# Row-wise infinity norm: another plan of tail loads, and the first load from two queues

## The chip, the cores and the metric

The kernel runs on one core of a Trainium2 chip. The metric is the device time of one execution in microseconds, lower being better. Three executions of the kernel before gave 629.21, 629.24 and 629.35 us; their median is 629.24 us.

## The reference

The input is a float32 matrix of 8192 rows and 8192 columns. The output has one float32 for each row: the largest absolute value in it.

```python
def setup_inputs():
    return {"x": np.random.randn(8192, 8192).astype(np.float32)}

def reference(x: np.ndarray) -> np.ndarray:
    return np.linalg.norm(x, ord=np.inf, axis=1)
```

The kernel reads 268.44 MB from HBM once and writes 32 KB.

## The kernel before

Loads are issued by SyncE's DMA queue, the reductions run on VectorE, a few combinations of partial results on GpSimd. ScalarE and TensorE do nothing.

**Two parts of the matrix.** The last 18 x 128 rows are the tail (`ROWS = 18`): each of the 128 partitions holds 18 consecutive rows, one after another, so that a partition's part is a line of 147456 elements. All rows before are the big part, in 23 steps: in each step a partition gets two whole rows, so a load has 128 partitions x 16384 elements (8 MB). `x_big` and `x_tail` are these views.

**The ring.** The loads go into one SBUF buffer, `ring`, of 3 x 16384 elements per partition, with 2048 elements apart from it (`APART`) for the pieces of the last row. `Pieces.room` hands out places in the ring one after another and begins again at the start when the rest is too short. A load may only start when the reductions that read its place are done, and when the reduction eight loads before is done, since the eight semaphores (`SEMS`) each count one load at a time. So up to three big loads are in SBUF: one being reduced and two landing or waiting on the queue.

**Loads and reductions.** `Pieces.load` (the DMA is line 90 of the profile) issues a load and adds 16 to its semaphore when it has landed. `Pieces.reduce` (line 108) issues the `tensor_reduce` with the absolute maximum over each row, or piece of a row, of the load. Its first instruction waits for the load's semaphore; VectorE takes the loads in their order. In the big part one instruction reduces two rows into `res_big`.

**The plan of the tail.** `tail_loads` cuts the line of 18 rows into loads that become smaller toward the end. It works backward from the last load, whose width is `FIRST` columns, with a linear cost for a load (`LOAD`, us per column and us per load) and for a reduction (`REDUCE`); each earlier load is made about as wide as lets its reduction be done when the next load has landed. Widths are multiples of `GRAIN` = 64; `SNAP` moves a cut to the end of a row where that is near. The last piece of row 16 is loaded late, just before the last piece of row 17. In the kernel before the tail has 25 loads, the first of 16384 columns, the last ones of 1984, 1920, 1664, 1472, 1280 and 1152 columns.

**Partial results.** A row in several pieces gets a partial maximum for each. For rows 0 to 16 GpSimd combines them (line 205) into `res_tail`. For row 17 the partial results are written behind the last piece in the ring, so that the last reduction reads 1152 + 4 elements and needs no combination.

**The end.** Three stores go out on SyncE's queue. `early` (line 218, `res_big`) and `middle` (line 222, the first 16 tail rows) wait for the reduction before last. The final store (line 235, rows 16 and 17 of the tail) waits for GpSimd's last combination and for the last of six one-element memsets (`IDLE`, line 216), which stand behind the last reduction on VectorE.

Of the kernel before, what the change touches and what calls it, by code (L numbers as in the profile page):

```python
# [7 lines left out]
P = 128  # L8
# [3 lines left out]
SEMS = 8  # L12


LOAD = (1.1775e-3, 0.075)
REDUCE = (1.0417e-3, 0.060)
ROWS = 18
FIRST = 1152
SNAP = 0.7
GRAIN = 64  # L20

IDLE = 6


def tail_loads(n_cols, big):

    slack = 0.0
    lag = REDUCE[0] * FIRST + REDUCE[1]
    loads = []
    end = ROWS * n_cols

    def take(top, bottom, most):
        nonlocal slack
        w = 0  # L40
        n = 0
        while True:

            n += 1
            start = max(bottom, (top - 1) // n_cols * n_cols - (n - 1) * n_cols)
            fit = int((lag + slack - REDUCE[1] * n) / REDUCE[0])
            w = max(w, min(fit, top - start) // GRAIN * GRAIN)
            if fit <= top - start or start <= bottom:
                break
        w = max(GRAIN, min(w, most, top - bottom))  # L50
        row = (top - w + n_cols - 1) // n_cols * n_cols
        if top - row >= SNAP * w or (w == most and top > row):
            w = top - row
        n = (top - 1) // n_cols - (top - w) // n_cols + 1
        slack += (LOAD[0] - REDUCE[0]) * w + LOAD[1] - REDUCE[1] * n
        loads.append((top - w, w))
        return top - w

    ends = [take(end, end - n_cols, FIRST), take(end - n_cols, end - 2 * n_cols, n_cols)]
    for top, bottom in zip(ends, (end - n_cols, 0)):  # L60
        while top > bottom:
            top = take(top, bottom, big)
    return loads[::-1]


class Pieces:
# [7 lines left out]
    def __init__(self, tc, ring):  # L74
        self.tc, self.nc, self.ring, self.head = tc, tc.nc, ring, 0
        self.sems = [tc.alloc_semaphore(f"loaded{i}") for i in range(SEMS)]
        self.started = self.reduced = 0
        self.last = []

    def room(self, w):  # L80
        if self.head + w > RING:
            self.head = 0
        at = self.head
        self.head += w
        return at

    def load(self, at, w, src):
        i = self.started
        self.started += 1
        ins = self.nc.sync.dma_start(out=self.ring[:, at : at + w], in_=src)  # L90
        ins.then_inc(self.sems[i % SEMS], 16)
        self.tc.no_tile_sem_insts.add(ins.ins.name)
        self.tc.declare_no_dep(ins.ins, group="loads", reason="a reduction stands in between")
        self.tc.add_to_no_dep_group("loads", ins.ins)
        if i >= SEMS:
            self.tc.add_manual_dep(
                ins.ins,
                self.last[i - SEMS].name,
                mybir.DependencyInfo(mybir.DependencyClass.Sync, mybir.DependencyReason.DATA),
                reason="the semaphore counts one load at a time",  # L100
            )

    def reduce(self, pairs):

        i = self.reduced
        self.reduced += 1
        for k, (dst, src) in enumerate(pairs):
            ins = self.nc.vector.tensor_reduce(  # L108
                out=dst,
                in_=src,  # L110
                axis=mybir.AxisListType.X,
                op=mybir.AluOpType.max,
                apply_absolute_value=True,
            )
            if k:
                self.tc.keep_in_program_order(ins)
            else:
                ins.wait_op(self.sems[i % SEMS], 16 * (i // SEMS + 1), "sem-ge")
            self.tc.declare_no_dep(ins.ins, group="loads", reason="waits on the load's semaphore")
        self.last.append(ins.ins)  # L120
        return ins
# [3 lines left out]
def kernel(  # L125
# [5 lines left out]
    nc = tc.nc  # L131
# [3 lines left out]
    tail = tail_loads(n_cols, R * n_cols)  # L135
    split = n_rows - ROWS * P
    n_big = split // (R * P)
# [8 lines left out]
    res_big = single.tile([P, n_big, R], f32)  # L146
    res_tail = single.tile([P, ROWS], f32)
    idle = single.tile([1, IDLE], f32)
    pieces = Pieces(tc, ring)

    for t in range(n_big):
        at = pieces.room(R * n_cols)
# [6 lines left out]
    for i, (start, w) in enumerate(tail):  # L159
        c = 0  # L160
        while c < w:
            row = (start + c) // n_cols
            n = min(w - c, (row + 1) * n_cols - start - c)
            parts.append((row, i, c, n))
            c += n
    of_row = [[q for q in parts if q[0] == row] for row in range(ROWS)]

    spots, behind, dst = {}, {}, {}  # L170
    at = RING
    for row, own in enumerate(of_row):
        if row == ROWS - 1:
            spots[own[-1][1]] = at
# [13 lines left out]
    for i, (start, w) in enumerate(tail):  # L188
        at = spots[i] if i in spots else pieces.room(w)
# [7 lines left out]
        )  # L197
        for row in range(ROWS - 1):
            if len(of_row[row]) > 1 and of_row[row][-1][1] == i:
                best = dst[of_row[row][0]]  # L200
                more = [dst[q] for q in of_row[row][1:]]
                while more:
# [3 lines left out]
                        out=to,  # L206
# [7 lines left out]
    tc.declare_fence(done.ins, group="loads")  # L214
    for i in range(IDLE):
        tc.keep_in_program_order(nc.vector.memset(idle[:, i : i + 1], 0.0))  # L216

    early = nc.sync.dma_start(
        out=out[:split].rearrange("(p q) -> p q", p=P), in_=res_big.rearrange("p t r -> p (t r)")
    )  # L220
    out_tail = out[split:].rearrange("(p r) -> p r", p=P)
    middle = nc.sync.dma_start(out=out_tail[:, : ROWS - 2], in_=res_tail[:, : ROWS - 2])
    for store in (early, middle):
        tc.add_manual_dep(
            store.ins,
# [2 lines left out]
            reason="not beside the last load",  # L228
# [37 lines left out]
```

## Time and profile before

| what | value |
|---|---|
| median of three runs | 629.24 us |
| time of the profiled execution | 629.17 us |
| its span in the profile | 627.4 us |
| VectorE busy | 551.9 us, 88% of the span, 62 instructions |
| reduction of 128x16384 (23 of them) | 17220 ns each |
| reduction of 128x8192 (9 in the tail) | 8677 ns each |
| last reduction, 128x1156 | 1347 ns |
| first load issued, first reduction starts | 0.72 us, 22.58 us |
| last load issued, final store issued | 609.34 us, 625.09 us |

The span is the time between the first and the last instruction that the profile records; the execution's own time is 1.77 us longer. Each DMA load is one instruction on SyncE's queue; its data moves on the core's 16 DMA engines, and the profile also records their packets. A reduction's busy time contains a part that overlaps with the next reduction: consecutive reductions start about 0.08 us before the one ahead has ended.

### The profile page before, as it was taken

To read this page: it belongs to the slowest core of one execution; us is meant where nothing else is said; L and a number is where in the kernel's file an instruction comes from. 1 tells how busy PE (TensorE), PEld (TensorE's weight loads), DVE (VectorE), ACT (ScalarE), POOL (GpSimd) and SP (SyncE) were. 2 spreads that over 40 slices of the span, in tenths; PEclk is the share of its full clock that TensorE was granted. 3 is DMA by queue.
4 is the path that set the end of the run, shared out by engine and by line. 5 is a ranking of instruction groups with operands and counts; after the bars stand their busy time and mean duration, and the time that the engine had idled before them with its cause. 6 is when DMAs were issued, how large, how long until landed. Compare 5 with 4: busy or idle time off the path is not lost.

```text
span 627.4 us, 170 instructions
## 1 busy us (share of the span) xinstructions
DVE 551.9 (88%) x62; POOL 2.9 (0%) x13
## 2 busy tenths in 40 slices
DVE  0588988889988889888898888988889899999998
POOL 0000000000000000000000000000000000000000
DMA  9999999999999999999999999999999999999997
GB/s 401 401 468 401 468 401 468 401 468 401 468 401 468 401 468 401 468 401 468 401 468 401 468 401 464 405 455 414 443 410 440 452 401 429 432 440 429 419 423 298
DMA packets 7345, 268.48 MB, mean 428 GB/s; under 512 B 1200, under 2 KB 1200, under 8 KB 1968
## 3 DMA queue, kind: packets, MB, share of 16 engines
q1 hardware_dynamic: 7344, 268.47, 99.3%
q14 instruction: 1, 0.01, 0.0%
HBM read 268.44 MB, written 0.03 MB: 428 GB/s over the span
## 4 chain that ended last, share of the span: by engine, by line
DMA 57%; DVE 42%; issue 0%; DVEq 0%; SPq 0%
DMA ring<-in_x_dram 57%; DVE res_big L108 22%; DVE parts L108 11%; DVE res_tail L108 8%; DVE ring L108 1%; DVEq L261 0%; SPq L90 0%; DVE idle L216 0%
## 5 line engine op out<-in xcount | busy, mean ns | idle before, releaser
L108 DVE TENSOR_REDUCE res_big<-ring 128x2 f32<-128x16384 f32 x23 | 396.1, 17220 | 69.4 <-DMA ring<-in_x_dram 69.4
L108 DVE TENSOR_REDUCE res_tail<-ring 128x1 f32<-128x8192 f32 (+1 forms) x10 | 78.9, 7944 | 2.1 <-DMA ring<-in_x_dram 2.1
L108 DVE TENSOR_REDUCE parts<-ring 128x1 f32<-128x3520 f32 (+17 forms) x19 | 69.8, 3735 | 1.7 <-DMA ring<-in_x_dram 1.7
L108 DVE TENSOR_REDUCE ring<-ring 128x1 f32<-128x1984 f32 (+3 forms) x4 | 7.7, 1975 | 0.0
L205 POOL TENSOR_SCALAR res_tail<-parts 128x1 f32<-128x1 f32 x8 | 2.3, 289 | 614.1 <-DVE parts L108 614.1
L205 POOL TENSOR_SCALAR parts<-parts 128x1 f32<-128x1 f32 x1 | 0.4, 354 | 7.0 <-DVE parts L108 7.0
L250 POOL MEMSET const-bfloat16-1.0<- 128x1 bf16 x1 | 0.1, 102 | 0.0
L250 POOL MEMSET const-uint8-127<- 128x1 uint8 x1 | 0.1, 101 | 0.0
L250 POOL MEMSET const-float32-0.0<- 128x1 f32 x1 | 0.1, 98 | 0.2 <-issue 0.2
L250 POOL MEMSET const-float32-1.0<- 128x1 f32 x1 | 0.1, 98 | 0.0
L216 DVE MEMSET idle<- 1x1 f32 x6 | 0.1, 59 | 0.0
## 6 DMA issues: line engine op xcount, KB each, us to landing
ring<-in_x_dram SPq DMA_DIRECT2D x3, 4096.0 KB, 41.9
ring<-in_x_dram SPq DMA_DIRECT2D x1, 7488.0 KB, 31.1
ring<-in_x_dram SPq DMA_DIRECT2D x1, 6368.0 KB, 35.4
ring<-in_x_dram SPq DMA_DIRECT2D x1, 5920.0 KB, 40.8
ring<-in_x_dram SPq DMA_DIRECT2D x1, 4800.0 KB, 32.8
ring<-in_x_dram SPq DMA_DIRECT2D x1, 3488.0 KB, 40.4
ring<-in_x_dram SPq DMA_DIRECT2D x1, 3104.0 KB, 39.2
ring<-in_x_dram SPq DMA_DIRECT2D x1, 2944.0 KB, 40.8
```

Of the source, the lines that this page charges most:

```text
L108: ins = self.nc.vector.tensor_reduce(out=dst, in_=src, axis=mybir.AxisListType.X, op=mybir.AluOpType.max, apply_absolute_value=True,)
L205: combined = nc.gpsimd.tensor_scalar(out=to, in0=best, scalar1=two[0], scalar2=two[1] if len(two) == 2 else None, op0=mybir.AluOpType.max, ...
L216: tc.keep_in_program_order(nc.vector.memset(idle[:, i : i + 1], 0.0))
L250: nc = _bacc.Bacc("TRN2", target_bir_lowering=False, num_devices=1)
```

## The change

Five things change:

- The constants of the plan: `LOAD` 0.075 to 0.073, `FIRST` 1152 to 768, `SNAP` 0.7 to 0.6, and a new `SPARE` of 0.08 us which is taken from the time that every load but the last is allowed for its reduction. The tail then has 29 loads, the first of 16384 columns, the last ones of 1600, 1472, 1344, 1152, 1024, 896, 768 and 704 columns.
- The first load of the kernel is issued as two DMAs: partitions 0 to 63 from SyncE's queue and partitions 64 to 127 from ScalarE's. Both add 16 to the same semaphore, and the counts to wait for are kept in `due`.
- `early` and `middle` are issued by ScalarE's queue. The final store stays on SyncE's.
- `IDLE` goes from six memsets to two.
- The number of instructions follows: 60 reductions for 56, one more combination on GpSimd, four more loads on SyncE's queue. Rows 16 and 17 come in 5 and 7 pieces, where they had 4 and 5, so the last reduction reads 704 + 6 elements.

```diff
-LOAD = (1.1775e-3, 0.075)
+LOAD = (1.1775e-3, 0.073)
 REDUCE = (1.0417e-3, 0.060)
+SPARE = 0.08
 ROWS = 18
-FIRST = 1152
-SNAP = 0.7
+FIRST = 768
+SNAP = 0.6
 GRAIN = 64
 
-IDLE = 6
+IDLE = 2
...
+        spare = SPARE if loads else 0
         while True:
...
-            fit = int((lag + slack - REDUCE[1] * n) / REDUCE[0])
+            fit = int((lag + slack - spare - REDUCE[1] * n) / REDUCE[0])
...
-        ins = self.nc.sync.dma_start(out=self.ring[:, at : at + w], in_=src)
-        ins.then_inc(self.sems[i % SEMS], 16)
-        self.tc.no_tile_sem_insts.add(ins.ins.name)
...
+        dst = self.ring[:, at : at + w]
+        queues = [(self.nc.sync, slice(0, P))]
+        if i == 0:
+
+            queues = [(self.nc.sync, slice(0, P // 2)), (self.nc.scalar, slice(P // 2, P))]
+        for queue, rows in queues:
+            ins = queue.dma_start(out=dst[rows], in_=src[rows])
+            ins.then_inc(self.sems[i % SEMS], 16)
+            self.counts[i % SEMS] += 16
+            self.tc.no_tile_sem_insts.add(ins.ins.name)
...
+        self.due.append(self.counts[i % SEMS])
...
-                ins.wait_op(self.sems[i % SEMS], 16 * (i // SEMS + 1), "sem-ge")
+                ins.wait_op(self.sems[i % SEMS], self.due[i], "sem-ge")
...
-    early = nc.sync.dma_start(
+    early = nc.scalar.dma_start(
...
-    middle = nc.sync.dma_start(out=out_tail[:, : ROWS - 2], in_=res_tail[:, : ROWS - 2])
+    middle = nc.scalar.dma_start(
+        out=out_tail[:, : ROWS - 2], in_=res_tail[:, : ROWS - 2]
+    )
```

More of the change, by code (lines that the diff above doesn't have):

```diff
@@ L78, in __init__ @@
         self.last = []
+        self.counts, self.due = [0] * SEMS, []
     def room(self, w):
@@ L89, in load @@
         self.started += 1
-        ins = self.nc.sync.dma_start(out=self.ring[:, at : at + w], in_=src)
-        ins.then_inc(self.sems[i % SEMS], 16)
-        self.tc.no_tile_sem_insts.add(ins.ins.name)
-        self.tc.declare_no_dep(ins.ins, group="loads", reason="a reduction stands in between")
-        self.tc.add_to_no_dep_group("loads", ins.ins)
+        dst = self.ring[:, at : at + w]
[7 more added lines that the diff above has]
+            self.tc.no_tile_sem_insts.add(ins.ins.name)
+            self.tc.declare_no_dep(ins.ins, group="loads", reason="a reduction stands in between")
+            self.tc.add_to_no_dep_group("loads", ins.ins)
+        self.due.append(self.counts[i % SEMS])
         if i >= SEMS:
```

## The prediction, made before the changed kernel was run

> **What bounds the kernel now.** I read the busy shares, then the DMA queues, then the chain of waits, then the groups of instructions with their waits, and last the stretches at both ends. From the page (parts 1 to 3):
>
> ```profile
> DVE 551.9 (88%) x62; POOL 2.9 (0%) x13
> ...
> DMA  9999999999999999999999999999999999999997
> ...
> q1 hardware_dynamic: 7344, 268.47, 99.3%
> ...
> HBM read 268.44 MB, written 0.03 MB: 428 GB/s over the span
> ```
>
> The DMA engines are busy in every slice (99.3% of the span), VectorE in 88%: the stream of loads is the bound. In the packet records a row of 64 KB takes one DMA engine 2.418 us, which is 27.1 GB/s, and 16 engines make 433.6 GB/s. The 268.44 MB then need 619.1 us at least; the span is 627.4, so 8.3 us lie outside the steady stream. A whole load of 128x16384 has eight such rows per engine, 8 x 2.418 = 19.34 us, and successive landings are indeed 19.35 us apart.
>
> The chain of waits, in order of time, says where the bound changes hands:
>
> ```profile
> 1.15 40.73 DMA ring<-in_x_dram
> 41.88 0.02 issue
> 41.91 17.23 DVE res_big L108
> ...
> 465.53 31.14 DMA ring<-in_x_dram
> 496.67 0.02 issue
> 496.69 7.22 DVE parts L108
> 503.91 17.19 DVE res_tail L108 x2
> 521.10 8.65 DVE parts L108 x2
> 529.75 34.37 DVE res_tail L108 x4
> 564.12 50.70 DVE parts L108 x14
> 614.83 7.58 DVE ring L108 x4
> 622.40 0.06 DVE parts L108
> ```
>
> Up to 496.67 the chain alternates between a load and its reduction (VectorE waits about 2.1 us for each load); from there to the end VectorE never waits. But it is only just late: the last load is issued at 609.34, lands 14.3 us later at 623.59, and its reduction starts at 623.72. So the DMA engines and VectorE end together: the widths of the tail loads are chosen so that each reduction is done about when the next load lands.
>
> The start, in stretches (width, VectorE and GpSimd busy, clock, DMA share, GB/s; a packet counts where it starts):
>
> ```profile
> 1.00:1.50 0.50, 0.00 (x0) 0.00 (x0) 1.00 0.00 0
> 1.50:2.00 0.50, 0.00 (x0) 0.00 (x0) 1.00 4.02 1311
> 2.00:2.50 0.50, 0.00 (x0) 0.00 (x0) 1.00 1.80 655
> 2.50:3.00 0.50, 0.00 (x0) 0.00 (x0) 1.00 0.31 131
> ```
>
> 1311 x 0.5 us is ten rows of 64 KB, 655 x 0.5 five, 131 x 0.5 one: the 16 engines start their first rows from 1.74 to 2.67 us, though SyncE issued at 0.72. These first rows take 2.51 to 3.49 us, not 2.42. Load 0 lands at 22.56.
>
> [...]
>
> **The change part by part.** The sum is made on the profiled execution (629.17 us, span 627.4, 1.8 outside it); the median, 629.24, is 0.07 above it.
>
> *Tail plan.* Intervals between landings in the tail fit 1.1766 ns per column plus 0.073 us per load (most within 0.008 us). Four more loads, with the same columns: the last landing moves by 4 x 0.073 = +0.29 us, to 623.88. The last reduction goes from 1156 columns (1.347 us) to 710; rows of 8192 (8.676) and 1156 give 1.0416 ns per column and 0.143, so 0.883 us: -0.464. VectorE's lag behind the last landing goes from 0.13 to 0.09. I stepped through both plans load by load (start = later of landing + 0.024 and VectorE free; 0.061 us net per reduction): before ends at 625.07 (the profile has 625.06), after at 624.85. **-0.22 us.** All other reductions, four more of them, are in that recurrence; their cover is the same 0.1 us lag behind the loads. GpSimd has one more combination (0.29 us) earlier, hidden: the last of them still follows the reduction before last and ends some 0.4 us before the final store.
>
> *Fillers, six to two.* The final store waits for the last memset. They start 0.007 to 0.01 us apart (625.004 to 625.039); four fewer: **-0.03 us**.
>
> *Stores on ScalarE's queue.* Both wait for the reduction before last, now at about 624.05. Issues of 0.35 and 0.43 us then run to about 624.9. On SyncE they would end right where the final store is due (624.87); on ScalarE nothing is queued behind them. They land after 1.5 and 1.7 us, the second at about 626.2, under the final store (624.87 + 1.5 = 626.35). If the cover of 0.15 fails, up to +0.2. I take 0. SyncE's issues in the tail (0.33 each, four more) wait for reductions as before, with several loads queued ahead of them (landing comes 14 us after the last issue): 0.
>
> *First load in two halves.* ScalarE leaves the opening barrier at 0.66 and is free at 0.73, against SyncE's issue at 0.72, so both queues fill together, and the issue on ScalarE (some 0.38 us) delays nobody. Load 1 sits behind the first half on SyncE's queue. The first reduction waits for both halves. What this does to the stream isn't shown in the trace; I bound it.
> - Lower end: each queue has 64 rows to describe instead of 128. If that is what staggers the starts (0.93 us), half of it goes: -0.46. If the queues share the describing, 0. I take -0.3 in this case.
> - Upper end: every engine alternates rows of the two halves. When all 16 engines have a row of the lower half, [...] each row takes twice 2.418; then all turn to the upper half[...]. Load 0 takes 128 / 8 x 2.418 = 38.7 us instead of 19.35: +19.3. [...] The spread of 0.93 us in the starts is small against a row of 4.8, so I see little that pulls the engines apart. I take **+17.5**[...].
>
> A delay of load 0 isn't absorbed later: each following load comes through queues that never run empty (99.3%), so every landing, and with it the end, moves by the delay of the slowest engine. VectorE just waits longer once.
>
> Sum with contention: -0.22 - 0.03 + 17.5 = +17.2 us, 646.4 from the median. Without: -0.25 - 0.3 = -0.55, 628.7.
>
> **The rivals.**
> 1. *Contention[...]* (57%): full, about 646.4 (own range 643 to 649; 42%), or partial, where engines get into opposite phase after some rows (631 to 643; 15%). For it: the bound is the DMA engines[...]. It decides from small doses: one row in eight at half speed on the slowest engine costs 2.4 us, more than the tail gives back. Against: [...] the two queues fill within 0.02 us of each other[...].
> 2. *No contention, small gain* (37%): 628.7, between 628.0 and 629.3. The queue interleaves finely or the engines fall into opposite phase at once. For it: the tail arithmetic is exact to 0.01 us on the kernel before, and the start has only 0.93 us of stagger to win.
> 3. *A larger gain at the start* (6%): the first rows at full speed from 1.74 for all engines would let load 0 land up to 1.1 us sooner (5.29 where the last first row ends, less 1.74 + 2.42); with the tail -1.35, 627.9.
> 4. That the tail plan misses its aim, with VectorE waiting for loads again, is inside all of these: each wait would show as at most 0.1 us.
>
> **How the numbers follow.** A measurement of this kernel can tell about 0.2%, 1.26 us, from no change: 627.98 to 630.50 count as the same. Contention in any dose lies above it (57%); the small gain lies within it (37%); the larger one under it (6%). The forecast is that of the likeliest case, 646.4. The range from 628.3 to 649.0 reaches from most of the small gain to full contention plus 2.6 us, and leaves out the larger gain, the edge of the small one and a worse contention, together under 2 in 10.
>
> **What would show it.** Contention: in the stretch from 1.7 to 40 us the DMA rate is near half of 433 GB/s, rows of the first load last up to 4.8 us in the packet records, and the first reduction starts near 40 us instead of 22.58; later landings are again 19.35 us apart. No contention: first reduction at 22.1 to 22.6. In both, the last reduction (128x710) takes 0.88 us, starts about 0.1 us after its landing, and VectorE has no idle time after its wait near 496 (or that plus the shift). I am wrong on the main point if load 0 lands by 23 us; on the tail, if VectorE waits for loads in its last 100 us, or if ScalarE's second store lands after the final one.

## The result, and the profile after

The changed kernel takes 649.68 us (median of four runs, 649.05 to 649.97) against 629.30 (629.21 to 629.45) beside it: a ratio of 1.0322, 95% interval 1.0307 to 1.0338, so 20.4 us slower. The profiled execution took 649.81 us with a span of 648.0. The forecast was 646.4 with a range to 649.0: the direction was right, and so was the place of the loss (the rows of the first load at about half their rate); the size was 3.2 us too small and the range ended 0.7 us too low.

The page of the changed kernel, parts 1 to 3:

```profile
DVE 552.1 (85%) x62; POOL 3.2 (0%) x14
...
DMA  9979999999999999998999999999899999999997
GB/s 194 259 259 453 445 396 453 453 396 445 453 433 409 453 445 396 453 453 388 453 453 417 425 453 441 400 453 453 388 453 432 417 439 432 419 444 421 425 423 292
...
q1 hardware_dynamic: 7568, 264.25, 96.2%
q10 hardware_dynamic: 368, 4.23, 3.1%
...
HBM read 268.44 MB, written 0.03 MB: 414 GB/s over the span
```

VectorE has as much work as before (551.9 us there). The new queue, q10, is ScalarE's: 4.19 MB of it are its half of the first load. The row to look at is GB/s: in the first three of 40 slices (16.2 us each) it is 194 to 259, while the busy row above it still shows 9, 9 and 7. In the kernel before it was 401 or more in every slice but the last:

```profile
GB/s 401 401 468 401 468 401 468 401 468 401 468 401 468 401 468 401 468 401 468 401 468 401 468 401 464 405 455 414 443 410 440 452 401 429 432 440 429 419 423 298
```

A row that takes twice as long (about 4.9 us instead of 2.42, below) is recorded as busy for all of that time: in the stretch from 10 to 20 us a DMA share of 0.98 goes with 210 GB/s here, and one of 1.04 with 452 in the kernel before. So a full busy row doesn't say how fast bytes move.

The changed kernel in finer stretches (columns as in the prediction: width, VectorE and GpSimd busy, clock, DMA share, GB/s):

```profile
1.50:2.00 0.50, 0.00 (x0) 0.00 (x0) 1.00 0.00 0
2.00:2.50 0.50, 0.00 (x0) 0.00 (x0) 1.00 9.39 1966
2.50:3.00 0.50, 0.00 (x0) 0.00 (x0) 1.00 0.65 131
...
5.00:10.00 5.00, 0.00 (x0) 0.00 (x0) 1.00 0.98 210
10.00:20.00 10.00, 0.00 (x0) 0.00 (x0) 1.00 0.98 210
20.00:30.00 10.00, 0.00 (x0) 0.00 (x0) 1.00 0.98 210
30.00:40.00 10.00, 0.00 (x0) 0.00 (x0) 1.00 0.98 210
46.00:60.00 14.00, 14.00 (x1) 0.00 (x0) 1.00 1.04 449
```

And one stretch of the kernel before:

```profile
10.00:20.00 10.00, 0.00 (x0) 0.00 (x0) 1.00 1.04 452
```

Until 40 us the rate is 210 GB/s, half of what follows, with a DMA share of 0.98. The first rows now start at 2.05 us, where they started at 1.74. In the packet records 16 rows of SyncE's half come first, as many as there are engines, then 16 of ScalarE's, and so on, eight turns, each row about 4.9 us long (means of 4.89 to 4.92, 5.02 in the first turn). The engines begin a turn within 1.1 us of one another, and this spread doesn't grow: both halves are being loaded at the same time for only a fifth of the time. From 44 us on, rows take 2.42 us again.

The chain of waits, in order of time:

```profile
0.72 42.44 DMA ring<-in_x_dram
43.16 0.03 issue
43.19 17.22 DVE res_big L119
60.41 1.71 another core or an unknown queue
62.12 0.02 issue
62.14 17.23 DVE res_big L119
79.37 0.02 issue
79.39 40.78 DMA ring<-in_x_dram
...
485.76 31.15 DMA ring<-in_x_dram
516.91 0.02 issue
516.93 6.75 DVE parts L119
...
643.46 0.06 DVE parts L119
643.52 0.70 issue
644.22 0.91 DVEq L274
645.12 0.01 DVE idle L227 x2
```

The end of the same chain before:

```profile
625.06 0.04 DVE idle L216 x6
```

(What ends at 62.12 is the wait for the second load, though the chain can't name its queue.) The first reduction starts at 43.19 instead of 22.58, the second at 62.14 instead of 41.91: 20.2 us late. After that the rhythm is the old one (40.78 for two loads in the chain, as before), and the last reduction ends at 645.12 instead of 625.06, 20.06 us late. So the loss stands complete at 62 us, and the tail gives back 0.2 us.

### The profile page after: what moved, and what is told of

It reads as the page before. It is cut to its first block, busy times and chain, and to the rows that moved or that the text cites. A ratio compares the mean times of both kernels' runs of the same rounds, so it can differ in the third digit from the quotient of the medians.

```text
span 648.0 us, 176 instructions
## 1 busy us (share of the span) xinstructions
DVE 552.1 (85%) x62; POOL 3.2 (0%) x14
## 4 chain that ended last, share of the span: by engine, by line
DMA 55%; DVE 43%; another core or an unknown queue 0%; issue 0%; DVEq 0%
DMA ring<-in_x_dram 55%; DVE res_big L119 24%; DVE parts L119 12%; DVE res_tail L119 7%; DVE ring L119 1%; DVEq L274 0%; DVE idle L227 0%
## 5 line engine op out<-in xcount | busy, mean ns | idle before, releaser
L119 DVE TENSOR_REDUCE parts<-ring 128x1 f32<-128x3136 f32 (+18 forms) x22 | 78.5, 3639 | 1.2 <-DMA ring<-in_x_dram 1.2
L119 DVE TENSOR_REDUCE res_tail<-ring 128x1 f32<-128x8192 f32 (+1 forms) x9 | 69.8, 7812 | 2.1 <-DMA ring<-in_x_dram 2.1
L119 DVE TENSOR_REDUCE ring<-ring 128x1 f32<-128x1600 f32 (+5 forms) x6 | 8.3, 1444 | 0.0
```

What stands on the lines that cost most here:

```text
L119: ins = self.nc.vector.tensor_reduce(out=dst, in_=src, axis=mybir.AxisListType.X, op=mybir.AluOpType.max, apply_absolute_value=True,)
```

## The experiments

The theories: **P**, while all engines write into partitions 0 to 63, or all into 64 to 127, each row takes about twice its time, the engines move in step from one half to the other, and a load with as many partitions in one half as in the other keeps its rate (the author's assumption, which the runs e1, e3, e4 and e5 put to the test); **Q**, two queues that take turns on the engines cost the time, whatever the partitions; **R**, any copy of fewer than 128 partitions is slow. A smaller question was where the rest of the change, forecast at -0.25 us, goes; theory **S** is that the two stores on ScalarE's queue are still in flight when the final store goes out, and hold it up.

**The split alone** (e1).

```diff
# against the kernel before, in load()
+        if i == 0:
+            queues = [(sync, rows 0 to 63), (scalar, rows 64 to 127)]
```

> The kernel before with the first load in two halves of 64 partitions from two queues, and nothing else of the change. Theory P ([...] all engines are in the same half at the same time): first reduction near 43 us, rows of the first load 4.9 us, time 649.5 (+20.2). If instead the tail plan or the stores carry a visible part of the loss, it would stay under 648.

Measured: 649.62 us (649.44 to 649.99) against 629.13; ratio 1.0326 (1.0311 to 1.0342), +20.5. Rows of the first load take 4.95 us, and the first reduction starts at 43.81:

```profile
10.00:20.00 10.00, 0.00 (x0) 0.00 (x0) 1.00 0.99 210
...
43.81 17.22 DVE L121 TENSOR_REDUCE res_big<-ring 128x2 f32<-128x16384 f32 x1 [43.81 <-DMA ring<-in_x_dram]
```

The first line is from the stretches, the second from the timeline. The split makes the whole loss.

**Halves by columns, two queues** (e3). Same two queues, same bytes, but each DMA has all 128 partitions.

```diff
+            queues = [(sync, rows 0 to 127, columns 0 to 8191), (scalar, rows 0 to 127, columns 8192 to 16383)]
```

> The kernel before with the first load in two halves by columns (all 128 partitions, 8192 columns each) from SyncE's and ScalarE's queues. Theory P: rows of 32 KB at full speed (1.21 us), first reduction at 22.3 to 23.0 us, time 629.0 to 629.8. Theory Q (two queues that take turns on the engines cost the time, whatever the partitions): as slow as the change, about 649.

Measured: 629.24 us against 629.13; ratio 1.0001 (0.9993 to 1.0010), no difference. The stretches:

```profile
1.50:2.00 0.50, 0.00 (x0) 0.00 (x0) 1.00 2.69 721
2.00:2.50 0.50, 0.00 (x0) 0.00 (x0) 1.00 0.88 262
2.50:3.00 0.50, 0.00 (x0) 0.00 (x0) 1.00 0.18 66
...
5.00:10.00 5.00, 0.00 (x0) 0.00 (x0) 1.00 1.09 472
10.00:20.00 10.00, 0.00 (x0) 0.00 (x0) 1.00 0.99 426
```

The rate is full from the beginning (426 to 472 GB/s after 5 us), and the packet records show the engines alternating between q1 and q10 every 1.21 us, a row of 32 KB. Q falls. The starts are still spread from 1.72 to 2.54, and the first reduction begins at 22.76, where it began at 22.58: a second queue doesn't shorten the start either.

**Halves by partitions, one queue** (e4).

```diff
+            queues = [(sync, rows 0 to 63), (sync, rows 64 to 127)]
```

> The kernel before with the first load in two halves of 64 partitions, both on SyncE's queue, one after the other. Theory P: rows 4.9 us, first reduction near 42.5 us, time 648.8 to 649.4. Theory Q: no second queue, so 629.3 with rows of 2.42 us.

Measured: 650.96 us (650.63 to 651.15); ratio 1.0346 (1.0331 to 1.0362), +21.8. The stretches:

```profile
1.50:2.00 0.50, 0.00 (x0) 0.00 (x0) 1.00 0.00 0
2.00:2.50 0.50, 0.00 (x0) 0.00 (x0) 1.00 7.48 1573
2.50:3.00 0.50, 0.00 (x0) 0.00 (x0) 1.00 2.24 524
...
5.00:10.00 5.00, 0.00 (x0) 0.00 (x0) 1.00 1.02 210
```

Half the rate without any second queue. With e1, e3 and the kernel before (one whole load) there are four cases: one queue or two, with and without halves by partitions. Only the partitions matter: with halves by partitions 649.62 us (two queues) and 650.96 (one), without them 629.24 and 629.13. It went past its expectation by 1.6 us: rows inside a half take 5.12 us, and only the one in which the engines change from the lower to the upper half takes 4.90. With two queues every row is such a change, and takes 4.9. In the changed kernel both halves are being loaded at the same time for a fifth of the time; that this is where the shorter row comes from fits and isn't shown.

**The middle half** (e5). 64 partitions in one DMA again, but other ones: 32 of the lower half and 32 of the upper.

```diff
+            queues = [(sync, rows 32 to 95), (scalar, rows 0 to 31), (scalar, rows 96 to 127)]
```

> The kernel before with the first load in three: partitions 32 to 95 from SyncE's queue, then 0 to 31 and 96 to 127 from ScalarE's. Theory P, [...] SyncE's rows take 2.42 us and ScalarE's 4.8 to 4.9; an engine needs 4 x 2.42 + 4 x 4.85 = 29.1 us for the load, 9.7 more than before: first reduction near 32.5 us, time 639 (637.5 to 641). Theory R (any copy of fewer than 128 partitions is slow, whichever they are): all rows near 4.9 us or slower, time 649 or more. Theory Q: about 649 too.

Measured: 641.42 us (640.77 to 643.82); ratio 1.0206 (1.0184 to 1.0228), +12.3; first reduction at 34.70. The stretches:

```profile
5.00:10.00 5.00, 0.00 (x0) 0.00 (x0) 1.00 1.02 210
10.00:20.00 10.00, 0.00 (x0) 0.00 (x0) 1.00 1.04 315
20.00:30.00 10.00, 0.00 (x0) 0.00 (x0) 1.00 0.85 229
```

R falls: a row of SyncE's 64 partitions that follows another such row takes 2.42 us, full speed, while ScalarE's rows of 32 partitions take 4.9 to 5.1 on average. The same run leaves out a rival on the side of HBM, that reading 64 rows so far apart is slow: by the view `x_big` the rows for partitions 32 to 95 have the same spacing there as those for 0 to 63, and half of them are the same rows. The sum was 2.2 us too small at the first reduction (34.70 against 32.5), because a fast row right after a slow one takes about 3.0 us (2.6 to 3.4): an engine's sequence, two slow, two fast, then slow and fast in turn, adds up on average to 4.96 + 5.11 + 3.05 + 2.45 + 4.89 + 3.00 + 4.91 + 2.94 = 31.3 us, where the expectation had 29.1.

**Half the dose** (e6). Only the first 8192 columns in halves, the rest as a whole load on SyncE's queue.

```diff
+            queues = [(sync, rows 0 to 63, columns 0 to 8191), (scalar, rows 64 to 127, columns 0 to 8191),
+                      (sync, rows 0 to 127, columns 8192 to 16383)]
```

> The kernel before with only the first 8192 columns of the first load in halves of 64 partitions from two queues (32 KB rows), and its other 8192 columns as a whole load on SyncE's queue: half the dose. Theory P: four rows of 32 KB per engine and half, eight in all at twice 1.21 us, then eight at full speed: +9.7 to +10.5 us, 639 to 640, first reduction at 32.5 to 33.5 us. If the loss were a fixed cost of starting a second queue, +20 as in the whole dose.

Measured: 638.78 us (638.70 to 638.93) against 629.14; ratio 1.0153 (1.0136 to 1.0169), +9.6; first reduction at 32.29. The loss goes with the bytes that are loaded in halves (+9.6 us for half of them, +20.5 for all in e1), and is no fixed cost of a queue. The whole-load part pulls the rate up in the second of these stretches:

```profile
10.00:20.00 10.00, 0.00 (x0) 0.00 (x0) 1.00 0.95 210
20.00:30.00 10.00, 0.00 (x0) 0.00 (x0) 1.00 0.91 370
```

It also bears on the rows of e4: here rows that follow one of their own half take 2.54 to 2.55 us on average, rows that follow one of the other half 2.32 to 2.33, and twice the full-speed row would be 2.43.

**The change without the split** (e2).

```diff
# against the changed kernel
-            queues = [(sync, rows 0 to 63), (scalar, rows 64 to 127)]
```

> The changed kernel with the first load whole, from SyncE's queue: the tail plan, two fillers and ScalarE's stores alone. Step of the prediction: -0.25, so 628.9, if the final store lands as fast as before (1.47 us after its issue). Theory S (the two stores on ScalarE's queue are still in flight when the final one goes out, and hold it up): the final store lands 0.5 us later, the gain is lost, 629.3 to 629.5.

Measured: 628.95 us (628.68 to 629.55) against 629.09; ratio 0.9997 (0.9989 to 1.0006): 0.14 us that the interval doesn't separate from nothing. The end of its timeline:

```profile
623.99 0.88 DVE L116 TENSOR_REDUCE res_tail<-ring 128x1 f32<-128x710 f32 x1
624.10 0.38 ACTq L226 DMA_DIRECT2D out_dram<-res_big  x1
624.25 0.36 POOL L213 TENSOR_SCALAR res_tail<-parts 128x1 f32<-128x1 f32 x1 [10.80 <-DVE parts L116]
624.52 0.55 ACTq L230 DMA_DIRECT2D out_dram<-res_tail  x1
624.81 0.06 DVE L224 MEMSET idle<- 1x1 f32 x2
624.90 0.35 SPq L245 DMA_DIRECT2D out_dram<-res_tail  x1
```

The last reduction ends at 624.87 (forecast 624.85), the final store goes out at 624.90 (forecast 624.87) and lands 1.43 us later. S finds nothing here.

**The stores alone on ScalarE's queue** (e7), and **the tail plan and fillers with all stores on SyncE's** (e8).

```diff
# e7, against the kernel before          # e8, against the changed kernel without the split
-    early = nc.sync.dma_start(           -    early = nc.scalar.dma_start(
+    early = nc.scalar.dma_start(         +    early = nc.sync.dma_start(
# and the same for middle in both
```

> The kernel before with its two early stores on ScalarE's queue, nothing else. Here the final store goes out 0.4 us later after the second store than in the changed kernel. Theory S: 0 to +0.3 us, 629.1 to 629.4. Without a collision: 629.1, unchanged.

> The changed kernel with the first load whole and all three stores on SyncE's queue: the tail plan and two fillers alone. By the prediction the second store's issue ends about when the final one is due, so the final store is issued 0 to 0.15 us late: 628.9 to 629.1. Theory S: as fast as or faster than the same with stores on ScalarE's queue. If the place on SyncE's queue matters more, it is slower than that one.

Measured: e7 629.16 us, ratio 1.0000 (0.9992 to 1.0008), unchanged. e8 629.26 us, ratio 1.0002 (0.9994 to 1.0010). Neither differs from the kernel before, but the end of e8's timeline shows what the move is for:

```profile
623.80 0.88 DVE L116 TENSOR_REDUCE res_tail<-ring 128x1 f32<-128x710 f32 x1
623.91 0.35 SPq L226 DMA_DIRECT2D out_dram<-res_big  x1
...
624.30 0.58 SPq L230 DMA_DIRECT2D out_dram<-res_tail  x1
624.62 0.06 DVE L224 MEMSET idle<- 1x1 f32 x2
625.00 0.36 SPq L245 DMA_DIRECT2D out_dram<-res_tail  x1
```

VectorE is done at 624.68, but the final store waits until 625.00: the second store's issue, 0.58 us here, ends at 624.88. With ScalarE's queue (e2) that wait is 0.03 us. The medians of e8 and e2, on one chip, differ by 0.31 us, which is less than the intervals above can separate; ten of e2's 13 runs, though, lie below every run of e8. The last reduction, 0.88 us from 623.80, is now too short to cover two issues on SyncE's queue (0.35 us from 623.91 and 0.58 from 624.30).

**Earlier stores** (e9).

```diff
# against the changed kernel without the split
-            pieces.last[-2].name,
+            pieces.last[-4].name,
```

> The changed kernel with the first load whole, and ScalarE's two stores waiting for the reduction four from the end instead of the last but one, so some 2 us earlier, beside the last loads. Theory S: the final store lands in 1.5 us again, 628.8 to 629.0, at best -0.35 against the kernel before; the two stores' packets (31 KB) may delay the last loads by up to 0.1 us. Without theory S: the same time as with the later stores.

Measured: 628.91 us (628.85 to 629.17), ratio 0.9998 (0.9990 to 1.0006), the same as e2. The final store lands 1.42 us after its issue, as in e2. This and e2 are the fastest versions tried, 20.7 us below the changed kernel, and not separable from the kernel before.

**The change and the split alone, side by side** (e10, e11). In the first profile of the changed kernel the final store landed 2.04 us after its issue, where all others had 1.4 to 1.5.

> The changed kernel once more, on the same chip as the split alone. If the rest of the change gives 0.14 us beside the split as it does without it, it is 0.1 to 0.2 us faster than the split alone. If the late landing of its final store (2.04 us after the issue, where the others had 1.4 to 1.5) belongs to the change with the split, it is 0.3 to 0.5 us slower than that, and the profile shows the late landing again; if that was one execution's, the store lands in 1.4 to 1.5 us.

> The kernel before with the first load in two halves alone, beside the changed kernel on one chip: 649.4 to 649.8 again; its rows of the first load 4.9 us, first landing between 43.1 and 43.8.

Measured: the change 649.34 us (648.98 to 649.72; ratio 1.0320, 1.0306 to 1.0334), the split alone 649.64 (649.57 to 649.84; 1.0326, 1.0312 to 1.0340). The final store landed after 1.51 us this time: the late landing belonged to one execution. The change is 0.3 us faster than the split alone, which fits the tail's 0.2 but is within the scatter of the runs.

## Why the prediction was right or wrong

- **What bounds the kernel**: right. A delay of the first load reached the end almost whole (20.2 us at the second landing, 20.1 at VectorE's end), since the later loads came no faster than before (40.78 us for two in the chain, in both kernels).
- **Contention**: right in kind, and in its fullest dose. The rival without contention is out, and so is the partial one: the engines stayed in step through all eight rows (the starts of a turn within 1.1 us), as the small spread of the starts suggested. That the partitions written set the rate is shown: rows into 0 to 63, into 64 to 127, and into the quarters 0 to 31 and 96 to 127 took about 4.9 to 5.1 us, rows into 32 to 95 and into 0 to 127 took 2.42 after another such row. That rows into one half would take twice 2.418 was the author's assumption, since the trace of before has no such load. What the partitions of a half share was not shown.
- **The term that was mis-sized**, and so the step that failed, is the delay of the first load: taken as +17.5, it measured 20.2 us at the second landing. +17.5 was the author's estimate, 1.8 under the +19.3 of eight rows at exactly twice 2.418 us, and nothing in the trace of before showed that gain. I took it although my own argument was that nothing pulls the engines apart. Here a half alone ran at 205 GB/s (16 x 64 KB in the 5.12 us of e4), and two halves in turn at 214 (4.90 us): a gain of 4.5%, but both lie under 216.8, half of the 433.6 of whole loads.
- **Where the 20.2 us come from**, averaged over the 16 engines of the packet records: the first rows start 0.23 us later. The eight rows of load 0 take 19.3 us more (1.95 for the first, which had taken 3.07 us before and not 2.42, and 2.48 for each of the other seven). The first row of load 1 takes 0.51 us more (2.93 instead of 2.42). Together 20.0. That 19.3 is also the upper bound of the prediction is luck: it had counted neither the slow first row before nor rows above twice 2.418. The profiled execution came out 3.4 us above the sum: 2.7 from this term, 0.6 from the late landing of its final store (see e10), 0.1 from the tail.
- **The later start and the first row of load 1** were missing from the bounds. For the start I had allowed only a gain: the earliest row starts at 2.05 us instead of 1.74, the last at 2.65, as before (2.67). A DMA of partitions 0 to 63 takes SyncE 0.55 us to issue instead of 0.38, with one queue (e4) as with two, so it isn't the second queue. Load 1's rows start between 41.00 and 42.23, while other engines are still in the last row of ScalarE's half; that this is what slows them fits and isn't shown.
- **Earlier start from two queues** (-0.46 to 0): none in e3, whose two queues start no earlier (1.72 us, 1.74 before).
- **Tail plan and fillers**: the instants are right to 0.03 us (e2's profile). The time gained 0.14 us of the 0.25, and its interval doesn't separate that from nothing. **Stores**: no collision (e2, e7), as forecast. e8 shows about 0.3 us for leaving them on SyncE's queue, where I had counted the last issue as just in time: the second store's issue took 0.58 us instead of 0.43.
- **The range** ended at 649.0, only 0.7 us above the estimate's own upper end (629.24 - 0.25 + 19.3 = 648.3). That left too little for rows above twice the time, a later start and the first row of load 1.

## What to carry to other kernels

In these runs the partitions that a DMA wrote decided its rate: splitting this load by columns kept the full rate (629.24 us against 629.13), splitting it into the lower and the upper 64 partitions halved it to 210 GB/s, with one queue (e4, 650.96 us) as with two (e1, 649.62). The load stood at the head of a stream that is bound by DMA (99.3% of the span in the kernel before), and of its delay of 20.2 us at the second landing 20.1 arrived at the end of VectorE's work. Look at GB/s beside the busy share of the DMA engines, and at the length of single rows: the share stayed at 0.98 while half the bytes moved.

## What the runs showed of the hardware that was not expected

- The 64 partitions from 32 to 95 go at full speed (2.42 us for a row of 64 KB after another such row), those from 0 to 63 at half (4.9 to 5.1). So the number of partitions alone didn't set the rate.
- Halves in turn from two queues are a little faster per row (4.90 us) than one half after the other on one queue (5.12): 1.3 us between the medians of e1 and e4.
- Issuing the first load as 64 partitions took longer (0.55 us) than as 128 (0.38) or 32 (0.37, e5), and the first packet started 1.3 us after the issue began instead of 1.0. In the changed kernel the issue of load 1 behind it, with 128 partitions, took longer too (0.56 us instead of 0.43). No run here shows why.
- The first row after the slow load was slow too: 2.93 us for load 1's first rows after the halves, 2.42 from the second on.
